# Down pass of three MLP blocks: splits and weight sums all on VectorE, residual rows partly loaded in place, last norm scaled in place

## Chip, core and metric

The kernel runs on one core of one Trainium2 chip. The time is the device time of one execution in microseconds (us). TensorE (PE) does the matmuls into PSUM, VectorE (DVE), ScalarE (ACT) and GpSimd (POOL) do elementwise work, SyncE (SP) issues the DMAs. Each engine works through its own queue in order.

## What is computed

The reference runs three blocks one after the other over an array x of 1024 tokens by 1024 features. Each block is a mixer (attention, recurrence or convolution), an output projection and an MLP with 4096 hidden features; a norm stands behind the last.

```python
# second block; the first has biases b1, b2 and layer norms, the third is built like the second
x = x + mix @ w_out[l]
h = rms_norm_2(x, norm_mlp_g[l])
x = x + jnp.square(jax.nn.relu(h @ w_mlp_up[l])) @ w_mlp_down[l]
...
out = rms_norm_3(h, norm_final_w)      # behind the third block
```

The change touches only the product with w_down (the "down pass") of each of the three MLPs, the step into it, and the final norm.

## The kernel before

`out_mlp` (L1104) is called three times. Every fp32 matrix is kept as a pair, a high part `hi` (a cast by ACT) and a low part `lo = x - hi` (a subtraction), and one product is three matmuls (`mm3`, L219 to L221). Both MLP products are done by a scheme of seven products in place of eight: each operand is a 2 by 2 block matrix, and the seven products take sums of blocks.

The down pass is 28 **stages** j. Stage j belongs to chunk c = j // 7 of the hidden features (four chunks) and to product s = j % 7. A stage has four **tiles** t of 128 tokens, and a tile is 12 matmuls of 128x512 (four k, three matmuls each), so a stage is 48 matmuls. A stage needs:

- its hidden operand `H[j]`, a tile of 1 MB loaded from DRAM two stages ahead by `hload` (L1229) and split in two halves g = 0, 1 by `hsplit` (ACT cast L1234, subtraction L1235). Before, half 0 was subtracted by VectorE and half 1 by GpSimd;
- its weights `W2[j, g]`, split by `wsplit`, which calls `parts` (ACT cast L1100, subtraction on VectorE L1101, written into `wlo`). Products s = 2 to 6 use sums of weight blocks made by `wsums` (L1259 to L1264). The four blocks of a chunk come by `wload` (L1246), 4 MB. `wsums` runs in stages s = 0, 1, 2: eight subtractions of 128x1024 in each chunk. GpSimd did them, apart from the four of the first chunk's s = 0, which VectorE did.

The results lie in PSUM: products s = 0, 2, 4, 6 in the wide tiles `d`, the others in `m` and `s`. `evict(j, t)` adds tile t to X in SBUF (VectorE, L1376); the first one into each place copies with ACT instead (L1379). X has eight rows of 128x1024; a stage adds into rows 0 to 3 or 4 to 7. A matmul of tile t = 2 or 3 in a `d` stage waits for the eviction of tile t - 2 of the same stage. The residual rows `xres` are added in stages s = 3 to 6 of chunks 1 and 2, one row a stage (load L1437, GpSimd add L1438; the first MLP also adds its bias row b2, L1440).

The order of every queue, SyncE's too, is the order in which the code emits the work, forced by `ordered(...)`. Before, `hsplit` and the first `wsplit` of stage j + 1, and all `wsums`, are emitted behind tile 0 of stage j and before that tile's eviction; `wsplit(j + 1, 1)` comes behind tile 1.

The step into the down pass is the 16th round (p = 15) of the up pass, whose last sums (`after(15, 6)`, L1208 to L1213, six instructions on ACT and GpSimd) run during stage 0.

In the last MLP, `done(t, x)` is called behind the evictions of stages 26 and 27, once for each row: square and sum on ACT (L1452, into a scratch tile `st` or `t`), a small step on VectorE (L1453), the power -1/2 on GpSimd (L285), the scaling on VectorE (L1458, written over the scratch tile), and the store to DRAM (L2345). `pipe` runs the square of row t, then the store of row t - 2 and the scaling of row t - 1. There is one `st` and one `t`, used in turn, so the square of row t waits for the store of row t - 2.

Of the kernel before, what the change touches and what calls it, by code (L numbers as in the profile page):

```python
# [102 lines left out]
class K:  # L103
# [1000 lines left out]
    def out_mlp(self, w_out, alpha, norm, w1, b1, w2, b2, done, nxt=None):  # L1104
# [126 lines left out]
        def hsplit(j, g, e):  # L1231
            if j < 28:
                hi, lo = (H[j][:, n, 2 * g : 2 * g + 2] for n in range(2))
                A.copy(hi, f32v(lo))  # L1234
                e.tensor_tensor(lo, f32v(lo), f32v(hi), op=ALU.subtract)  # L1235
# [17 lines left out]
        def wsums(c, s, g):  # L1253

            b11, b12, b21, b22 = w2r[c, g]
            if s == 0:
                t2[g] = (self.st if g else self.t4)().rearrange("p (a b) -> p a b", a=2)
                e = P if c else V
                e.tensor_tensor(b11, b12, b11, op=ALU.subtract)  # L1259
                e.tensor_tensor(t2[g], b22, b11, op=ALU.subtract)  # L1260
            elif s == 1:
                P.tensor_tensor(b12, b22, b12, op=ALU.subtract)
            elif s == 2:
                P.tensor_tensor(b21, b21, t2[g], op=ALU.subtract)  # L1264
# [30 lines left out]
        with self.ordered(("PE", "Activation", "DVE", "Pool", "SP"), False):  # L1295
# [32 lines left out]
            for p in range(1, 16):  # L1328
                for n in range(0 if p > 1 else 2, 7):
# [22 lines left out]
                    else:  # L1352
# [6 lines left out]
                        elif n == 4:  # L1359
                            hsplit(0, 0, V)  # L1360
                            hsplit(0, 1, P)
                            wsplit(0, 0)
                            hload(2)
                        elif n == 5:
                            wsplit(0, 1)
# [6 lines left out]
            def evict(j, t):  # L1372
                q = into[j % 7]
                x = half(q[0], t, q[1])
                if (t, q) in begun:
# [5 lines left out]
            for j in range(28):  # L1381
# [3 lines left out]
                for t in range(4):  # L1385
# [13 lines left out]
                    if t == 0:  # L1399
# [8 lines left out]
                        hsplit(j + 1, 0, V)  # L1408
                        wsplit(j + 1, 0)
                        hsplit(j + 1, 1, P)  # L1410
                        if s < 3:
                            for g in range(2):
                                wsums(c, s, g)
                    if t == 1:
                        wsplit(j + 1, 1)

# [14 lines left out]
                if c in (1, 2) and s >= 3:  # L1431

                    t = 4 * (c - 1) + s - 3
                    if b2 is not None and t == 0:
                        b2t = self.gbtile(b2, self.g3())
                    r = self.slot("qa", [128, 1024], F32)
                    nc.sync.dma_start(out=r, in_=xr[:, t])  # L1437
                    P.tensor_tensor(X[:, t], X[:, t], r, op=ALU.add)  # L1438
                    if b2 is not None:
                        P.tensor_tensor(X[:, t], X[:, t], b2t, op=ALU.add)  # L1440
        self.qp.release()

    def rms_stages(self, t, x, g, end=None):
# [13 lines left out]
        def scale():  # L1457
            nc.vector.scalar_tensor_tensor(out=L["y"], in0=x, scalar=L["rs"], in1=g, op0=ALU.mult, op1=ALU.mult)  # L1458
# [937 lines left out]
```

## Time and profile before

| what | value |
|---|---|
| median of 3 runs | 3884.6 us (3877.1 to 3891.63) |
| the profiled execution's own time | 3888.89 us |
| its span, first to last instruction | 3887.2 us |
| mean granted TensorE clock | 0.952 of full |
| busy share of the span: PE, DVE, POOL, ACT | 91%, 61%, 45%, 39% |
| down passes, stages 0 to 25, three of them | 320.40, 310.70 and 311.09 us |

The three down passes lie at 1185 to 1516, 2350 to 2669 and 3526 to 3870 us of the span. Times below are us from the start of the span. A stage's start is the start of its first matmul in TensorE's timeline. In the rows, `X L1376` is an eviction, `wlo L1101` a weight split, `p L1235` or `q L1235` a split of the hidden operand.

### The profile page before, as it was taken

Reading aid. Unit: us, or ns where it says so; the run is one execution under the profiler, and the core shown is the slowest. Engines: PE = TensorE matmul, PEld = TensorE weight load, DVE = VectorE, ACT = ScalarE, POOL = GpSimd, SP = SyncE. Lnnn points to the kernel's source line nnn. Section 1 sums busy time; section 2 is a strip of 40 time slices with the busy share of each in tenths; the row PEclk is TensorE's granted clock in tenths of the full one; section 3 lists DMA queues with packets and bytes.
Section 4 is the critical chain, followed back from the end, with each engine's and each line's share of the span. In section 5 each row is a group of like instructions: output and inputs, shape, how many; then the busy total and the mean of one; then the engine's idle time right before and its main releaser. Section 6 shows DMA issues by size and latency. Waiting matters only on the chain.

```text
span 3887.2 us, 46771 instructions
## 1 busy us (share of the span) xinstructions
PE 3530.0 (91%) x17908; PEld 2877.7 (74%) x17908; DVE 2376.4 (61%) x3261; ACT 1515.4 (39%) x2485; POOL 1732.0 (45%) x1105
## 2 busy tenths in 40 slices
PE   8898898978999997868989999998999989999997
PEld 7777776766887776667767887776888867887775
DVE  7676534465556777797655556776445345556775
ACT  3333334443444333446733334333422233334332
POOL 2011103255555775577625555673112125555664
PEclk9998898989999998988999999999999999999998
DMA  4221235124456442310124446431111323445442
GB/s 159 63 52 52 61 114 193 60 74 127 150 156 215 154 157 87 78 42 23 38 83 130 150 156 217 168 136 65 48 55 44 104 71 122 150 150 211 152 152 92
DMA packets 335108, 438.51 MB, mean 113 GB/s; under 512 B 44459, under 2 KB 213864, under 8 KB 334244
## 3 DMA queue, kind: packets, MB, share of 16 engines
q1 hardware_dynamic: 331428, 429.23, 33.8%
q10 hardware_dynamic: 3456, 6.29, 0.4%
q8 instruction: 141, 2.31, 0.2%
q14 instruction: 83, 0.68, 0.1%
HBM read 298.62 MB, written 136.84 MB: 112 GB/s over the span
## 4 chain that ended last, share of the span: by engine, by line
PE 62%; DVE 16%; DMA 6%; issue 6%; POOL 5%; ACT 5%; SPq 1%; POOLq 0%; DVEq 0%; ACTq 0%
PE d L219 10%; PE d L221 10%; PE d L220 10%; PE s L219 4%; PE s L220 4%; PE s L221 4%; PE m L219 3%; PE m L220 3%; PE m L221 3%; DVE wlo L1101 3%; DMA L<-Ld 1%; DVE wlo L206 1%; PE s L2187 1%; DVE X L1376 1%; DVE acc L1592 1%
## 5 line engine op out<-in xcount | busy, mean ns | idle before, releaser
L219 PE MATMUL d<-p,whi 128*128 128x512 f32 x960 | 378.1, 394 | 38.9 <-DVE X L1201 27.0
L221 PE MATMUL d<-p,wlo 128*128 128x512 f32 x960 | 370.2, 386 | 4.7 <-DVE wlo L206 4.7
L220 PE MATMUL d<-p,whi 128*128 128x512 f32 x960 | 369.8, 385 | 3.4 <-POOL p L1081 3.4
L219 PE MATMUL d<-whi,p 128*128 128x512 f32 (+1 forms) x864 | 338.7, 392 | 35.4 <-DVE X L1376 25.5
L285 POOL TENSOR_TENSOR col<-col,mhalf 128x1 f32<-128x1 f32 (+2 forms) x132 | 128.8, 977 | 516.1 <-DVE col L1453 221.7
L1183 POOL TENSOR_TENSOR X<-X 128x512 f32<-128x512 f32 x144 | 169.3, 1176 | 400.1 <-ACT X L1182 400.1
L220 PE MATMUL d<-wlo,p 128*128 128x512 f32 (+1 forms) x864 | 327.5, 379 | 9.6 <-DVE wlo L206 8.7
L221 PE MATMUL d<-whi,p 128*128 128x512 f32 (+1 forms) x864 | 326.3, 378 | 2.0 <-DVE p L985 1.3
L219 PEld LDWEIGHTS d<-p,whi 128*128 128x128 f32 x960 | 182.7, 190 | 81.9 <-DVE X L1201 30.9
L219 PEld LDWEIGHTS d<-whi,p 128*128 128x128 f32 x864 | 171.8, 199 | 95.6 <-DVE X L1376 39.4
L1235 POOL TENSOR_TENSOR p<-p 128x1024 fp32r<-128x1024 f32 x54 | 171.0, 3169 | 143.3 <-ACT p L1234 47.8
L1101 DVE TENSOR_TENSOR wlo<-q,whi 128x1024 fp32r<-128x1024 f32 x72 | 214.2, 2975 | 10.2 <-ACT whi L1100 10.2
L1182 ACT ACTIVATE X<-X 128x512 f32<-128x512 f32 x144 | 91.0, 632 | 321.6 <-DVE X L1194 132.8
L221 PEld LDWEIGHTS d<-p,wlo 128*128 128x128 f32 x960 | 182.7, 190 | 43.3 <-DVE wlo L206 5.5
L220 PEld LDWEIGHTS d<-p,whi 128*128 128x128 f32 x960 | 183.0, 191 | 41.2 <-POOL p L1081 4.2
L1101 DVE TENSOR_TENSOR wlo<-raw,whi 128x1024 fp32r<-128x1024 f32 (+1 forms) x90 | 134.3, 1492 | 127.7 <-ACT whi L1100 127.7
L220 PEld LDWEIGHTS d<-wlo,p 128*128 128x128 f32 x864 | 172.3, 199 | 34.6 <-DVE wlo L206 9.4
L221 PEld LDWEIGHTS d<-whi,p 128*128 128x128 f32 x864 | 172.1, 199 | 31.5 <-DVE p L985 2.7
L1100 ACT CAST whi<-q 128x1024 fp32r<-128x1024 f32 x72 | 75.6, 1050 | 298.9 <-PE d L221 163.5
L206 DVE TENSOR_TENSOR wlo<-raw,whi 128x1024 fp32r<-128x1024 f32 (+3 forms) x91 | 121.3, 1337 | 82.1 <-ACT whi L206 81.7
L1376 DVE TENSOR_TENSOR X<-X,d 128x512 f32<-128x512 f32 x156 | 105.1, 680 | 107.7 <-PE d L221 107.7
L220 PE MATMUL m<-wlo,p 128*128 128x512 f32 (+2 forms) x416 | 150.4, 361 | 14.3 <-DVE wlo L1101 14.3
(635 smaller groups left out, 10319.4 us busy)
## 6 DMA issues: line engine op xcount, KB each, us to landing
hd<-X SPq DMA_DIRECT2D x48, 1280.0 KB, 4.8
p<-hd SPq DMA_DIRECT2D x108, 512.0 KB, 4.4
raw<-in_w_in_dram SPq DMA_DIRECT2D x62, 512.0 KB, 4.0
q<-hd SPq DMA_DIRECT2D x60, 512.0 KB, 4.5
hd<-X SPq DMA_DIRECT2D x48, 512.0 KB, 3.5
raw<-in_w_dram SPq DMA_DIRECT2D x32, 512.0 KB, 6.3
xres<-X SPq DMA_DIRECT2D x32, 512.0 KB, 2.6
raw<-in_w_mlp_up_dram SPq DMA_DIRECT2D x32, 512.0 KB, 6.3
```

Of the source, the lines that this page charges most:

```text
L206: self.split = nc.scalar.copy(hi, raw), nc.vector.tensor_tensor(lo, raw, f32v(hi), op=ALU.subtract), ld
L219: mm(out, ah, bh, start=first, stop=False, **kw)
L220: mm(out, ah, bl, start=False, stop=False, **kw)
L221: mm(out, al, bh, start=False, stop=last, **kw)
L285: self.nc.gpsimd.tensor_tensor(out, src, self.mhalf[:, :n], op=ALU.pow)
L1100: nc.scalar.copy(hi, x)
L1101: nc.vector.tensor_tensor(lo, x, f32v(hi), op=ALU.subtract)
L1182: A.activation(h, h, AF.Relu)
L1183: P.tensor_tensor(h, h, h, op=ALU.mult)
L1235: e.tensor_tensor(lo, f32v(lo), f32v(hi), op=ALU.subtract)
L1376: V.tensor_tensor(x, x, out[j, t], op=ALU.add)
L1592: V.scalar_tensor_tensor(out=ac[:, q : q + wd], in0=h[:, q + k : q + k + wd], scalar=cw[:, n, k : k + 1], in1=ac[:, q : q + wd], op0=ALU.m ...
```

## The change

- `hsplit` does all its subtractions on VectorE, and half 1 is emitted behind tile 1 of the stage, not behind tile 0.
- `wsums` runs on VectorE alone, and is emitted behind tiles 2 and 3, so behind the splits of the next stage.
- In the step into the down pass the two first weight splits are emitted one product later (n = 5 and 6, not 4 and 5).
- Residual rows 4 to 7 are loaded by two DMAs of 1 MB straight into X during stage 2, so the first evictions into those rows add (VectorE) and do not copy (ACT). Rows 0 to 3 are still loaded aside and added by a new function `addend`, on VectorE, behind tile 2; the bias row of the first MLP is added on VectorE behind tile 3.
- The last norm scales X in place and stores from X. The scratch tile is then free as soon as its square is done.

```diff
@@ -1228,11 +1228,11 @@
                         c = 4 * (j // 7) + 2 * g
                         nc.sync.dma_start(out=f32v(H[j][:, 1, 2 * g : 2 * g + 2]), in_=hd[j % 7, :, c : c + 2])
 
-        def hsplit(j, g, e):
+        def hsplit(j, g):
             if j < 28:
                 hi, lo = (H[j][:, n, 2 * g : 2 * g + 2] for n in range(2))
                 A.copy(hi, f32v(lo))
-                e.tensor_tensor(lo, f32v(lo), f32v(hi), op=ALU.subtract)
+                V.tensor_tensor(lo, f32v(lo), f32v(hi), op=ALU.subtract)
 
         def wload(c):
             if c < 4:
@@ -1255,13 +1255,27 @@
             b11, b12, b21, b22 = w2r[c, g]
             if s == 0:
                 t2[g] = (self.st if g else self.t4)().rearrange("p (a b) -> p a b", a=2)
-                e = P if c else V
-                e.tensor_tensor(b11, b12, b11, op=ALU.subtract)
-                e.tensor_tensor(t2[g], b22, b11, op=ALU.subtract)
+                V.tensor_tensor(b11, b12, b11, op=ALU.subtract)
+                V.tensor_tensor(t2[g], b22, b11, op=ALU.subtract)
             elif s == 1:
-                P.tensor_tensor(b12, b22, b12, op=ALU.subtract)
+                V.tensor_tensor(b12, b22, b12, op=ALU.subtract)
             elif s == 2:
-                P.tensor_tensor(b21, b21, t2[g], op=ALU.subtract)
+                V.tensor_tensor(b21, b21, t2[g], op=ALU.subtract)
+
+        def addend(c, s, n):
+
+            nonlocal b2t
+            t = 4 * (c - 1) + s - 3
+            if n == 0 and t < 4:
+                r = self.slot("qa", [128, 1024], F32)
+                nc.sync.dma_start(out=r, in_=xr[:, t])
+                V.tensor_tensor(X[:, t], X[:, t], r, op=ALU.add)
+            elif n == 1 and b2 is not None:
+                if t == 0:
+                    b2t = self.gbtile(b2, self.g3())
+                V.tensor_tensor(X[:, t], X[:, t], b2t, op=ALU.add)
+
+        b2t = None
 
 
         first = None
@@ -1357,11 +1371,12 @@
                         elif n == 3:
                             hload(1)
                         elif n == 4:
-                            hsplit(0, 0, V)
-                            hsplit(0, 1, P)
-                            wsplit(0, 0)
+                            hsplit(0, 0)
+                            hsplit(0, 1)
                             hload(2)
                         elif n == 5:
+                            wsplit(0, 0)
+                        elif n == 6:
                             wsplit(0, 1)
 
             half = lambda q, t, c: X[:, 4 * q + t, 512 * c : 512 * c + 512]
@@ -1372,7 +1387,7 @@
             def evict(j, t):
                 q = into[j % 7]
                 x = half(q[0], t, q[1])
-                if (t, q) in begun:
+                if (t, q) in begun or q[0] == 1:
                     V.tensor_tensor(x, x, out[j, t], op=ALU.add)
                 else:
                     begun.add((t, q))
@@ -1405,14 +1420,18 @@
                             wload(1)
                         if s == 0 and c:
                             wload(c + 1)
-                        hsplit(j + 1, 0, V)
+                        hsplit(j + 1, 0)
                         wsplit(j + 1, 0)
-                        hsplit(j + 1, 1, P)
-                        if s < 3:
-                            for g in range(2):
-                                wsums(c, s, g)
-                    if t == 1:
+                    elif t == 1:
+                        hsplit(j + 1, 1)
                         wsplit(j + 1, 1)
+                    elif s < 3:
+                        wsums(c, s, t - 2)
+                    elif c in (1, 2):
+                        addend(c, s, t - 2)
+                    if j == 2 and t in (1, 2):
+                        x = slice(2 * t + 2, 2 * t + 4)
+                        nc.sync.dma_start(out=X[:, x], in_=xr[:, x])
 
                     if j == 1 and t >= 2:
                         evict(0, 2 * t - 4)
@@ -1428,19 +1447,9 @@
                             else:
                                 self.XT[1] = self.xt_meta() if nxt == "meta" else self.xt_half(1)
                         done(t + 4 * (s - 5), X[:, t + 4 * (s - 5)])
-                if c in (1, 2) and s >= 3:
-
-                    t = 4 * (c - 1) + s - 3
-                    if b2 is not None and t == 0:
-                        b2t = self.gbtile(b2, self.g3())
-                    r = self.slot("qa", [128, 1024], F32)
-                    nc.sync.dma_start(out=r, in_=xr[:, t])
-                    P.tensor_tensor(X[:, t], X[:, t], r, op=ALU.add)
-                    if b2 is not None:
-                        P.tensor_tensor(X[:, t], X[:, t], b2t, op=ALU.add)
         self.qp.release()
 
-    def rms_stages(self, t, x, g, end=None):
+    def rms_stages(self, t, x, g, end=None, out=None):
 
         nc = self.nc
         XT = getattr(self, "XT", None)
@@ -1455,7 +1464,7 @@
             self.rpow(L["rs"], ss, 1)
 
         def scale():
-            nc.vector.scalar_tensor_tensor(out=L["y"], in0=x, scalar=L["rs"], in1=g, op0=ALU.mult, op1=ALU.mult)
+            nc.vector.scalar_tensor_tensor(out=L["y"] if out is None else out, in0=x, scalar=L["rs"], in1=g, op0=ALU.mult, op1=ALU.mult)
 
         return [square, scale, lambda: end(L["y"]) if end else self.to_xt(XT, t, L["y"])]
 
@@ -2342,7 +2351,8 @@
         def done(t, x):
             if t == 0:
                 G[1] = self.gbtile(i["norm_final_w_3"], self.g3())
-            self.pipe(*self.rms_stages(t, x, G[1], lambda y: nc.sync.dma_start(out=ov[:, t], in_=y)))
+            q, s, _ = self.rms_stages(t, x, G[1], out=x)
+            self.pipe(q, s, lambda: nc.sync.dma_start(out=ov[:, t], in_=x))
 
         self.out_mlp(i["w_out_3"][0], 1.0, self.rms_feed("norm_mlp_w_3"), i["w_up_3"][0], None, i["w_down_3"][0], None, done)
         self.flush()
```

In each down pass 28 hidden splits and 28 of the 32 weight sums leave GpSimd's queue and stand in VectorE's, with the added rows. The lines of the kernel after shift a little: `wsums` is L1258 to L1263, the eviction L1391, the scaling L1467.

VectorE, third MLP, from the first hidden split for stage 1 on. L1235 is a hidden split, L1101 a weight split, L1259 and L1260 (before) or L1258 and L1259 (after) are weight sums. Before:

```order
L1235 TENSOR_TENSOR p_3784_25725<-p_3784_25725 128x1024
L1101 TENSOR_TENSOR wlo_25811<-q_3782_25687,whi_25810 128x1024
L1259 TENSOR_TENSOR q_3782_25687<-q_3782_25687 128x2x512
L1260 TENSOR_TENSOR t_3794_25816<-q_3782_25687 128x1024
L1259 TENSOR_TENSOR p_3783_25688<-p_3783_25688 128x2x512
L1260 TENSOR_TENSOR st_25819<-p_3783_25688 128x1024
L1101 TENSOR_TENSOR wlo_25835<-p_3783_25688,whi_25834 128x1024
```

And after, the same place:

```order
L1101 TENSOR_TENSOR wlo_25791<-q_3774_25667,whi_25790 128x1024
L1235 TENSOR_TENSOR p_3776_25705<-p_3776_25705 128x1024
L1101 TENSOR_TENSOR wlo_25809<-p_3775_25668,whi_25808 128x1024
L1258 TENSOR_TENSOR q_3774_25667<-q_3774_25667 128x2x512
L1259 TENSOR_TENSOR t_3788_25824<-q_3774_25667 128x1024
L1258 TENSOR_TENSOR p_3775_25668<-p_3775_25668 128x2x512
L1259 TENSOR_TENSOR st_25839<-p_3775_25668 128x1024
```

The four weight sums stood ahead of the second weight split (wlo of the p tile) and now stand behind it; the second hidden split, which was GpSimd's, stands between the two weight splits.

VectorE, third MLP, stages 26 and 27: the end of the kernel's down pass with the first rows of the norm. L1453 and L1462 are the small step, L1458 and L1467 the scaling. Before:

```order
L1235 TENSOR_TENSOR q_3976_27613<-q_3976_27613 128x1024
L1101 TENSOR_TENSOR wlo_27683<-q_3894_26819,whi_27682 128x1024
L1376 TENSOR_TENSOR X_5269<-X_5269,s_27530 128x512
L1453 TENSOR_SCALAR col_27692<-col_27692 128x1
L1101 TENSOR_TENSOR wlo_27710<-p_3895_26820,whi_27709 128x1024
L1376 TENSOR_TENSOR X_5269<-X_5269,m_27555 128x512
L1453 TENSOR_SCALAR col_27715<-col_27715 128x1
L1458 SCALAR_TENSOR_TENSOR st_27691<-X_5269,col_27695,g_3983_27689 128x1024
L1376 TENSOR_TENSOR X_5269<-X_5269,s_27573 128x512
```

And after:

```order
L1101 TENSOR_TENSOR wlo_27653<-q_3886_26801,whi_27652 128x1024
L1391 TENSOR_TENSOR X_5269<-X_5269,s_27500 128x512
L1462 TENSOR_SCALAR col_27660<-col_27660 128x1
L1235 TENSOR_TENSOR q_3964_27583<-q_3964_27583 128x1024
L1101 TENSOR_TENSOR wlo_27680<-p_3887_26802,whi_27679 128x1024
L1391 TENSOR_TENSOR X_5269<-X_5269,m_27523 128x512
L1462 TENSOR_SCALAR col_27685<-col_27685 128x1
L1467 SCALAR_TENSOR_TENSOR X_5269<-X_5269,col_27663,g_3971_27657 128x1024
L1391 TENSOR_TENSOR X_5269<-X_5269,s_27543 128x512
```

The second hidden split now stands between the small step of the first row and the second weight split, and the scaling writes X in place of `st`.

## Rows read from the trace of the kernel before

**Rows 1.** The page: busy time, share of the span and instructions by engine.

```profile
PE 3530.0 (91%) x17908; PEld 2877.7 (74%) x17908; DVE 2376.4 (61%) x3261; ACT 1515.4 (39%) x2485; POOL 1732.0 (45%) x1105
```

**Rows 2.** Windows, stages 0 to 25: us; PE, PEld, DVE, ACT, POOL busy; PEclk; DMA; GB/s.

```profile
1184.86:1505.26 320.40, 297.70 (x1250) 237.98 (x1249) 232.44 (x170) 115.27 (x125) 221.25 (x76) 0.97 0.44 158
2349.57:2660.27 310.70, 293.94 (x1250) 235.59 (x1248) 227.31 (x170) 115.02 (x125) 199.89 (x68) 0.98 0.43 156
3526.38:3837.47 311.09, 294.31 (x1250) 235.86 (x1249) 226.93 (x170) 115.11 (x125) 200.48 (x68) 0.98 0.43 156
```

**Rows 3.** Windows, third pass: stages 1, 2, 3 and 9, same columns.

```profile
3537.57:3558.07 20.50, 13.48 (x49) 10.62 (x48) 17.59 (x8) 7.14 (x10) 14.26 (x5) 0.83 0.89 320
3558.07:3568.96 10.89, 10.89 (x49) 9.01 (x48) 6.02 (x6) 3.61 (x5) 8.20 (x3) 1.00 0.31 98
3568.96:3580.16 11.20, 11.20 (x50) 9.02 (x49) 4.74 (x3) 6.04 (x8) 2.63 (x1) 1.00 0.28 94
...
3635.09:3650.16 15.07, 13.01 (x50) 10.11 (x49) 11.75 (x10) 4.11 (x6) 15.06 (x5) 0.89 0.20 70
```

**Rows 4.** Waits of TensorE, third pass to the end: total, times, longest.

```profile
PE d L219 <- DVE X L1376: 17.4, 16, 7.2
PE s L220 <- DVE wlo L1101: 7.0, 1, 7.0
PE d L219 <- DVE X L1201: 1.3, 1, 1.3
```

**Rows 5.** Timeline of TensorE in stage 1: start, duration, [idle before <- who ended it].

```profile
3546.34 0.79 PE L220 MATMUL s<-wlo,p 128*128 128x512 f32 x1 [7.02 <-DVE wlo L1101]
...
3547.36 0.63 PE L219 MATMUL s<-whi,p 128*128 128x512 f32 x1
```

**Rows 6.** Timeline of VectorE, stages 0 and 1 of the third pass.

```profile
3529.30 1.47 DVE L1235 TENSOR_TENSOR p<-p 128x1024 fp32r<-128x1024 f32 x1 [2.40 <-ACT p L1234]
...
3532.93 2.31 DVE L1259 TENSOR_TENSOR q<-q 128x1024 f32<-128x1024 f32 x1
...
3542.92 3.37 DVE L1101 TENSOR_TENSOR wlo<-p,whi 128x1024 fp32r<-128x1024 f32 x1
```

**Rows 7.** Timeline of GpSimd, same place.

```profile
3528.64 1.04 POOL L1209 TENSOR_TENSOR X<-X 128x512 f32<-128x512 f32 x1
3529.76 2.17 POOL L1210 TENSOR_TENSOR X<-X 128x512 f32<-128x512 f32 x1
...
3538.60 6.61 POOL L1235 TENSOR_TENSOR p<-p 128x1024 fp32r<-128x1024 f32 x2
```

**Rows 8.** Instructions of line 1235: duration in ns, min/median/max, by engine.

```profile
L1235 DVE TENSOR_TENSOR p<-p x54: 1216/1226/3393, 1188.3 to 3826.7; 128x1024 fp32r<-128x1024 f32 x54
L1235 POOL TENSOR_TENSOR p<-p x54: 2393/3326/3405, 1197.3 to 3826.8; 128x1024 fp32r<-128x1024 f32 x54
```

**Rows 9.** Timeline of VectorE: stage 26 and the last eviction.

```profile
3839.41 3.42 DVE L1101 TENSOR_TENSOR wlo<-q,whi 128x1024 fp32r<-128x1024 f32 x1
3842.75 0.67 DVE L1376 TENSOR_TENSOR X<-X,s 128x512 f32<-128x512 f32 x1
...
3846.85 0.68 DVE L1376 TENSOR_TENSOR X<-X,m 128x512 f32<-128x512 f32 x1
...
3876.40 0.68 DVE L1376 TENSOR_TENSOR X<-X,d 128x512 f32<-128x512 f32 x1
```

**Rows 10.** The chain that ended last, one row of the last norm: start, us, what.

```profile
3850.14 2.65 DMA out_dram<-st
...
3852.88 1.16 ACT st L1452 x2
3854.06 0.15 DVE col L1453
3854.21 1.20 DVE t L1458
```

**Rows 11.** Landing of the residual rows' loads (L1437).

```profile
DMA to landing us min/median/max: 5.2/5.3/6.6
```

## The prediction, made before the changed kernel was run

> **What bounds the kernel now.** I read the page first: TensorE is busy for 91% of the span, VectorE 61%, GpSimd 45% [rows 1]. So a gain has to come out of the 9% in which TensorE waits, and the change can reach only the waits in the three down passes, in the step into them and in the last norm. Next I cut each down pass out by windows, from the first matmul of stage 0 to the first of stage 26: 320.40, 310.70 and 311.09 us [rows 2]. Then I cut single stages. An undisturbed stage takes 10.89 us, or 11.20 us where the hidden operand lies in `q`; TensorE is then busy throughout (stages 2 and 3) [rows 3]. Of the 26 stages, 9 are of the `q` kind (every third), so a pass without waits is 17 x 10.89 + 9 x 11.20 = 285.9 us. The three passes stand 34.5, 24.8 and 25.2 us above that, 84.5 us together. This sum is what the change can win in the passes.
>
> Where it lies: stage 1 takes 20.50 us, 9.6 too many [rows 3]. TensorE waits 7.02 us in it for one weight split [rows 5], and afterwards its matmuls take 0.63 us each and the mean granted clock of the stage is 0.83: it works for a while at the lower of its two clocks, 1.2 GHz, and the wait of 7.0 costs 9.6 [rows 3, 5]. The other passes have the like in stage 1, so about 29 of the 84.5 us are these three waits. The rest, some 56 us, is spread over the `d` stages: TensorE waits at `d` tiles for VectorE's evictions [rows 4]; stage 9 with 15.07 us is one of them [rows 3].
>
> Who is late, and why: VectorE does the same subtraction of 128x1024 in 1.22 us at best and in 3.39 at worst, GpSimd in 2.39 to 3.41 [rows 8]. The long ones lie side by side. While GpSimd does sums of 128x512, which take 1.04 by themselves and 2.17 here, VectorE's weight sum takes 2.31, about 1.22 + 1.04; beside GpSimd's splits of the hidden operand (6.61 for two) its weight split takes 3.37 [rows 6, 7]. Each seems to wait for the other's instruction. The page "SBUF — State Buffer" of the Trainium skill (Who interferes with whom) says so: VectorE with two SBUF inputs and GpSimd share a port pair, whoever starts first holds it for its whole instruction, and the other blocks. By that rule work that leaves GpSimd gives VectorE its 1.22 us back at once; the rows agree. In stage 9 GpSimd is busy for 15.06 of the 15.07 us and TensorE for 13.01; in stage 3 GpSimd is busy for 2.63 and nothing waits [rows 3].
>
> **The change part by part.**
>
> *Stage 1.* Before, four weight sums stand ahead of the weight split that TensorE waits for, at 2.3 to 3 us each [rows 6]. After, they stand behind it. I follow the new queue from the hidden split at 3529.30 [rows 6], whose start is set by a load and does not move. Four splits lie there: hidden, weight, hidden, weight. GpSimd's last sums of the up pass stay where they are and last until about 3536 to 3538, so I take 2.31 for each: done by 3538.5. Stage 1 begins at 3537.57 [rows 3] and needs this split half a tile in, about 1.4 us later. Enough, by half a microsecond; with the sums of GpSimd over sooner, by two. I take the whole wait as gone, 9.6 us a pass, 29 in all; if it were late by one full instruction, 3 us a pass would come back with it. The four sums come next, then the splits for stage 2: eight instructions at 1.22 us are 9.8 us, done before stage 2 needs them.
>
> *Step into the pass.* The first weight splits come one product later. Hidden splits no longer go to GpSimd, so the eviction L1201, for which TensorE waits 1.3 us [rows 4], is early. But the second weight split now stands behind ACT's work on the next eviction and comes about as much late for stage 0. I count nothing; the bounds are -1.3 and +1.3 us a pass.
>
> *The other stages.* In stage j VectorE now does four splits for stage j + 1 and four evictions: 4 x 1.22 + 4 x 0.68 = 7.6 us [rows 8, 9]. In s = 1 and s = 2 two weight sums come on top (10.0 us), in s = 0 four (12.5 us), in s = 3 to 6 of chunks 1 and 2 one or two added rows (8.8 to 10.0 us). The rows' durations overlap a little at their ends, so these are upper values. Only s = 0 exceeds the stage's 10.89 us, by 1.6, and the next two stages take it back. TensorE's waits inside a stage need the eviction of tile 0 before tile 2 starts, 5.4 us into the stage: VectorE has the last eviction of the stage before (0.68), two splits (2.44) and this eviction (0.68) to do, 3.8 us. Before, the weight split alone took 3.42 there, beside GpSimd's [rows 9]. The sums come behind tiles 2 and 3, where no matmul of the same stage waits. So these waits go too; I leave 4 us of them for the three passes. No row shows a weight sum on VectorE without GpSimd beside it: the bounds are 1.22 (the split of the same size) [rows 8] and 2.31 [rows 6]. I take 1.22, since the operation, the size and the engine are the same.
>
> *Residual rows.* Twelve loads remain, and now VectorE waits for them in place of GpSimd. A load is issued about 1 us into the stage and lands 5.3 us later [rows 11]; the addition stands behind the eviction of tile 1, which TensorE allows at 5.5. Behind it are the evictions of tiles 2 and 3, for which nobody waits before the next `d` stage. Cost nothing; if the loads came late, 12 times up to 5.3 us, 64 us. The rows 4 to 7 come as 2 MB in stage 2, where DMA is used to 0.31 [rows 3], and are first added in stage 3. The eight evictions a pass that ACT did cost VectorE 8 x 0.68 us in stages 3 and 6; in stage 3 it is busy for 4.74 of 11.20 [rows 3].
>
> *Last norm.* Before, a row goes round in 2.65 (store) + 1.16 (square) + 0.15 + 1.20 (scaling of the row before) and small gaps, 5.27 us, and each square waits for a store [rows 10]. After, it waits for the eviction alone: eviction 0.68, square 1.16, 0.15, scaling 1.20, in all 3.2 us with the gaps. Stage 26 as before: the eviction of tile 0 at 3842.75 [rows 9] comes at 3840.6, since the weight split falls from 3.42 to 1.22; the second hidden split (1.22, and ACT's cast ahead of it, now behind the first square) goes in between; the eviction of tile 1 comes at about 3845.9, where it was at 3846.85 [rows 9]. Six rounds of 3.24 later the last eviction is at 3865.3, where it was at 3876.40 [rows 9]. Behind it all is as before. Gain 11 us. In the first two MLPs the norms behind the pass begin 1 us earlier each for the same reason: 2 us.
>
> *Sum.* 84.5 - 4 + 11 + 2 = 93.5 us. The profiled execution took 3888.89 us, which would become 3795; the median of the runs shown lies 4.3 us below it, so I forecast **3791 us**.
>
> **The rivals.**
>
> *The wait in stage 1 stays.* GpSimd's sums of the up pass are not moved and lie beside exactly these splits. If they stretch the splits past 3539, the wait shrinks but the lower clock comes back with it. Against: half a microsecond or more of room. Without these 29 us the time is 3820.
>
> *Weight sums cost 2.31 on VectorE by themselves.* Then s = 0 comes to 16.8 us and s = 1, 2 to 12.2; the lateness at the `d` stage s = 2 reaches 7.2 us and TensorE waits some 4.7 us there, in twelve chunks 56 us: 3847. For: every row of them is long. Against: each of those rows has GpSimd beside it.
>
> *Residual loads hold VectorE up.* With all of the 64 us above, 3855. Against: 5.3 us [rows 11] fit ahead of the addition.
>
> *VectorE becomes the bound, and the kernel slower.* If the long durations were VectorE's own and not GpSimd's doing, four splits at 3.39 and four evictions would take 16.3 us a stage, 5.4 above TensorE's 10.89; over 78 stages 420 us, about 4300. It decides from a mean of 2.04 us for a split, (10.89 - 2.72) / 4. The page "Perfetto Trace Analysis" (Optimizing Scalar/DVE Operations) gives the rule behind such a fear: where VectorE is saturated, moving work to ScalarE or even GpSimd may help; VectorE is busy for 73% of a pass [rows 2] and this change does the opposite. The same page adds that the shared port may undo it. Against: 1.22 us in the rows whenever GpSimd is idle.
>
> **How the numbers follow.** Forecast 0.74, stage 1 stays 0.11, long weight sums or slow loads 0.09, VectorE the bound 0.03, something else near no change 0.03. Faster by over 0.5% (about 19 us, what a measurement of this kernel can tell from none) holds for all but the last two: 0.94; within 0.5% 0.03; slower 0.03. The range: upwards it takes in the wait of stage 1 (3820) and 2 us of spread between runs, so 3822; downwards the 4 us that I left, 1.3 us a pass in the step, and a run some 7 us below the median, as those shown are: 3775.
>
> **What would show it.** VectorE's L1235, L1101, L1258 to L1263 all near 1.22 us in the passes, but for stage 0; GpSimd idle between the last sum of the up pass and the norm. The stages 0 to 25 at about 287 us a pass; no wait over 1 us at `wlo`. In the end rounds of about 3.2 us and no `out_dram` in the chain but for the last. It would be wrong if the splits stay long without GpSimd beside them, if stage 1 still runs at a granted clock below 1, or if VectorE waits for `qa` or X loads with TensorE waiting behind it.

## The result, and the profile of the changed kernel

| | before | after |
|---|---|---|
| median of the comparison | 3886.59 us (4 runs, 3877.1 to 3891.63) | 3769.85 us (4 runs, 3766.07 to 3780.07) |
| profiled execution | 3888.89 us, span 3887.2 | 3767.91 us, span 3766.2 |
| stages 0 to 25, three passes | 320.40, 310.70, 311.09 us [rows 2] | 287.20, 287.11, 287.12 us |
| start of stage 26 to the end of the span | 49.7 us | 36.2 us |

The ratio is 0.9707, 95% interval 0.9679 to 0.9734: faster, by more than forecast. 3769.85 lies 21 us below the 3791 of the prediction and 5 below its range.

The page's first line, then windows over stages 0 to 25 of the three passes and over single stages of the third (0, 1, 9), answer to [rows 1, 2, 3]:

```profile
PE 3483.8 (93%) x17908; PEld 2855.3 (76%) x17908; DVE 2364.7 (63%) x3473; ACT 1504.9 (40%) x2461; POOL 1121.7 (30%) x905
...
1167.86:1455.06 287.20, 286.36 (x1250) 234.22 (x1249) 233.85 (x244) 112.72 (x118) 9.59 (x6) 1.00 0.50 178
2294.05:2581.16 287.11, 286.35 (x1249) 234.21 (x1248) 224.22 (x236) 112.45 (x117) 9.69 (x6) 1.00 0.47 171
3442.91:3730.03 287.12, 286.36 (x1250) 234.23 (x1249) 225.54 (x236) 112.42 (x117) 10.58 (x6) 1.00 0.48 172
...
3442.91:3455.39 12.48, 11.71 (x50) 8.94 (x48) 9.44 (x5) 6.95 (x8) 10.58 (x6) 1.00 0.91 338
3455.39:3466.29 10.90, 10.90 (x49) 9.01 (x48) 10.83 (x11) 7.00 (x9) 0.00 (x0) 1.00 1.00 354
...
3544.00:3555.19 11.19, 11.19 (x49) 9.02 (x48) 9.38 (x12) 4.04 (x6) 0.00 (x0) 1.00 0.27 94
```

VectorE does 236 to 244 instructions in a pass where it did 170, and is busy for no longer: 224 to 234 us against 227 to 232 [rows 2]. GpSimd's 200 to 221 us are 10. TensorE waits 0.8 us a pass, all in stage 0; the granted clock is 1.00 throughout.

The waits of TensorE in the third pass, and the instructions of L1235 (ns, min/median/max), answer to [rows 4, 8]:

```profile
PE d L220 <- DVE wlo L1101: 0.8, 1, 0.8
...
L1235 DVE TENSOR_TENSOR p<-p x108: 1216/1219/2317, 1173.2 to 3722.8; 128x1024 fp32r<-128x1024 f32 x108
L1235 DVE TENSOR_TENSOR q<-q x60: 1218/1218/1227, 1161.4 to 3735.9; 128x1024 fp32r<-128x1024 f32 x60
```

VectorE across stages 0 and 1 (timeline: start, duration), to be held against [rows 6]:

```profile
3451.20 2.32 DVE L1235 TENSOR_TENSOR p<-p 128x1024 fp32r<-128x1024 f32 x1
3453.44 2.31 DVE L1101 TENSOR_TENSOR wlo<-p,whi 128x1024 fp32r<-128x1024 f32 x1
3455.68 1.21 DVE L1258 TENSOR_TENSOR q<-q 128x1024 f32<-128x1024 f32 x1
3456.92 1.23 DVE L1259 TENSOR_TENSOR t<-q 128x1024 f32<-128x1024 f32 x1
```

The weight split for which TensorE waited 7 us is done 0.4 us into stage 1, still at 2.31 beside GpSimd's last sums. The weight sums behind it take 1.21 to 1.23.

### The profile page after: what moved, and what is told of

It reads as the page before. It is cut to its first block, busy times and chain, and to the rows that moved or that the text cites. A ratio compares the mean times of both kernels' runs of the same rounds, so it can differ in the third digit from the quotient of the medians.

```text
span 3766.2 us, 46503 instructions
## 1 busy us (share of the span) xinstructions
PE 3483.8 (93%) x17908; PEld 2855.3 (76%) x17908; DVE 2364.7 (63%) x3473; ACT 1504.9 (40%) x2461; POOL 1121.7 (30%) x905
## 3 DMA queue, kind: packets, MB, share of 16 engines
q8 instruction: 141, 2.31, 0.3%
## 4 chain that ended last, share of the span: by engine, by line
PE 73%; DVE 11%; ACT 4%; DMA 4%; issue 4%; POOL 3%; SPq 0%; POOLq 0%; DVEq 0%; ACTq 0%
PE d L219 13%; PE d L221 13%; PE d L220 13%; PE s L219 5%; PE s L221 5%; PE s L220 5%; PE m L219 4%; PE m L220 4%; PE m L221 4%; DMA L<-Ld 1%; PE s L2196 1%; DVE wlo L206 1%; DVE acc L1601 1%; POOL st L1595 1%; DVE t L1601 1%
## 5 line engine op out<-in xcount | busy, mean ns | idle before, releaser
L219 PE MATMUL d<-whi,p 128*128 128x512 f32 (+1 forms) x864 | 332.5, 385 | 8.4 <-DVE X L1727 3.6
L221 PE MATMUL d<-whi,p 128*128 128x512 f32 (+1 forms) x864 | 324.1, 375 | 2.3 <-DVE p L985 1.3
L1101 DVE TENSOR_TENSOR wlo<-raw,whi 128x1024 fp32r<-128x1024 f32 (+1 forms) x90 | 135.8, 1508 | 128.7 <-ACT whi L1100 128.7
L206 DVE TENSOR_TENSOR wlo<-raw,whi 128x1024 fp32r<-128x1024 f32 (+3 forms) x91 | 120.1, 1324 | 81.0 <-ACT whi L206 80.5
L1391 DVE TENSOR_TENSOR X<-X,d 128x512 f32<-128x512 f32 x168 | 114.8, 684 | 83.2 <-PE d L221 83.1
L1234 ACT CAST p<-p 128x1024 fp32r<-128x1024 f32 x108 | 113.4, 1050 | 118.1 <-DMA p<-hd 118.1
L206 ACT CAST whi<-raw 128x1024 fp32r<-128x1024 f32 (+3 forms) x91 | 94.1, 1040 | 155.8 <-PE d L220 46.2
L219 PE MATMUL m<-whi,p 128*128 128x512 f32 (+2 forms) x416 | 150.9, 363 | 1.5 <-DVE q L1066 1.0
```

What stands on the lines that cost most here:

```text
L206: self.split = nc.scalar.copy(hi, raw), nc.vector.tensor_tensor(lo, raw, f32v(hi), op=ALU.subtract), ld
L219: mm(out, ah, bh, start=first, stop=False, **kw)
L221: mm(out, al, bh, start=False, stop=last, **kw)
L1101: nc.vector.tensor_tensor(lo, x, f32v(hi), op=ALU.subtract)
L1391: V.tensor_tensor(x, x, out[j, t], op=ALU.add)
```

## The experiments

All times stand beside the kernel before on the same chip. Line numbers shift by a few lines from kernel to kernel (the eviction is L1376, L1390 to L1396). The passes column is the sum of stages 0 to 25 over the three passes; "tail" runs from the start of stage 26 to the end of the span.

| kernel | median us | ratio to before (95%) | passes us | tail us |
|---|---|---|---|---|
| before, again | 3875.48 | 0.9999 (0.9986 to 1.0012) | 941.9 | 49.7 |
| engine alone | 3904.36 | 1.0071 (1.0047 to 1.0094) | 986.2 | 48.5 |
| order, residual rows, norm; GpSimd still at work | 3843.23 | 0.9911 (0.9889 to 0.9933) | 931.0 | 37.4 |
| norm alone | 3863.95 | 0.9961 (0.9949 to 0.9973) | 942.0 | 37.4 |
| engine, sums behind | 3815.39 | 0.9816 (0.9792 to 0.9839) | 882.2 | 48.5 |
| after, again | 3769.63 | 0.9707 (0.9688 to 0.9727) | 861.4 | 36.2 |
| after + idle work on GpSimd | 3815.38 | 0.9826 (0.9804 to 0.9849) | 901.2 | 36.2 |
| after, one split back | 3770.75 | 0.9716 (0.9690 to 0.9743) | 861.5 | 36.2 |
| after, all rows loaded apart | 3770.88 | 0.9715 (0.9692 to 0.9737) | 861.4 | 36.2 |
| after + earlier splits, deeper norm | 3763.14 | 0.9691 (0.9671 to 0.9711) | 857.4 | 30.9 |
| the same, again | 3764.28 | 0.9694 (0.9674 to 0.9715) | 857.4 | 30.9 |

### The kernel before, again: where the base went wrong

No edit.

> The kernel before, unchanged, profiled once more. It asks whether the stretch of low clock in front of the passes (granted clock 0.50 from 410 to 430 us, TensorE busy throughout, 11 to 15 us lost) belongs to this kernel or to one execution. Theory A, chance: this execution shows 1.00 there, or shows the drop elsewhere, and its span lies 10 to 15 us off that of the first profile. Theory B, tied to the kernel: 0.50 again in the same place, pass 1 entered at 1185 us as before (1167.86 in the changed kernel). Passes either way 320, 311 and 311 us.

Windows of the first profile of before, then of this one, at 362 to 364, 364 to 366 and 410 to 420 us:

```profile
362.00:364.00 2.00, 2.00 (x10) 0.50 0.04 8
364.00:366.00 2.00, 2.00 (x8) 0.50 0.00 0
410.00:420.00 10.00, 10.00 (x96) 0.50 0.35 101
...
362.00:364.00 2.00, 2.00 (x15) 1.00 0.00 0
364.00:366.00 2.00, 2.00 (x15) 1.00 0.00 0
410.00:420.00 10.00, 9.62 (x83) 1.00 0.30 105
```

The columns are length, PE busy (count), granted clock, DMA share, GB/s. Theory A holds: the same program, span 3871.7 in place of 3887.2, and 14.4 of the 15.5 us lie in front of pass 1 (stage 0 at 1170.43, not 1184.86). Of 13 profiled executions four show the stretch at 0.50 near 405 to 432 us: two of kernels with the old passes, one with the sums behind, one of the fastest kernel. Of 44 runs of before, 29 took 3871 to 3880 us and 15 took 3884 to 3892, with none between. That the upper group is the stretch is likely but seen in two profiled runs only: 3888.89 us with it, 3873.47 without.

### The changed kernel, again

> The changed kernel once more, beside the kernel before on the same chip. The first comparison set a profile of before with 27 us at a granted clock of 0.50 in front of the passes against one of after without. Theory: that stretch comes and goes from one execution to the next whatever the kernel; then the median of before is near 3876 and that of after near 3766 to 3768 again, ratio 0.971 to 0.973, and passes of 287.1 to 287.2 us each. Rival: the change itself removes the stretch; then no execution of it ends 10 us or more above its fastest.

3769.63 us and passes of 287.1 to 287.2. The rival falls: one run of the first comparison ended 14 us above the fastest (3780.07 against 3766.07), and the stretch occurs in a profile of the fastest kernel, which holds the whole change.

### The engine alone

```diff
-                e = P if c else V
+                e = V
...
-                P.tensor_tensor(b12, b22, b12, op=ALU.subtract)      # the like for b21 and the added rows
+                V.tensor_tensor(b12, b22, b12, op=ALU.subtract)
...
-                        hsplit(j + 1, 1, P)
+                        hsplit(j + 1, 1, V)
```

> Of the change only the engine: all splits, weight sums and added rows go to VectorE, in the order of the kernel before; residual loads and the last norm as before. Theory A (the long VectorE instructions are two engines waiting for each other's): outside stage 0 the splits L1235 and L1101 and the weight sums take 1.22 us; the evictions of most stages are early, but the sums now stand in the queue ahead of the second weight split and the next evictions: four sums in s = 0 are 4.9 us, so stage 1 and the stages s = 1 and 2 keep a wait of some 2 to 4 us. About a third to two thirds of the 81 us of the passes: 3830 to 3860. Theory B (the durations are VectorE's own): splits stay near 2 to 3.4 us, VectorE becomes the bound, above 4000.

3904 us, 28 slower than before: outside both theories. The durations are as A says. Stage 7 of the third pass: VectorE's timeline, TensorE's matmul behind its wait, the stage's window, and last the same stage of the kernel before, from its second profile:

```profile
3618.18 1.22 DVE L1235 TENSOR_TENSOR p<-p 128x1024 fp32r<-128x1024 f32 x1
3619.32 1.22 DVE L1259 TENSOR_TENSOR q<-q 128x1024 f32<-128x1024 f32 x1
...
3622.96 1.22 DVE L1260 TENSOR_TENSOR st<-p 128x1024 f32<-128x1024 f32 x1
3624.11 0.68 DVE L1376 TENSOR_TENSOR X<-X,d 128x512 f32<-128x512 f32 x1
...
3624.84 0.80 PE L219 MATMUL d<-whi,p 128*128 128x512 f32 x1 [5.10 <-DVE X L1376]
...
3614.14:3633.09 18.95, 13.85 (x50) 10.86 (x48) 11.23 (x11) 6.45 (x8) 0.00 (x0) 0.82 0.76 277
...
3597.82:3608.81 10.99, 10.99 (x49) 8.93 (x48) 7.00 (x6) 5.33 (x6) 7.15 (x3) 1.00 0.91 333
```

Every split and every sum takes 1.22 us, GpSimd does nothing, and the stage is 8 us longer than before. Three splits and four sums stand ahead of the eviction of tile 0, which comes 10 us into the stage, while TensorE needs it at 5.4; TensorE waits 5.1 us, and the stage's mean granted clock falls to 0.82. I had counted on waits of 2 to 4 us in stage 1 and in the stages s = 1 and 2, not on one in s = 0 itself, and left out what the clock adds. Stages 7, 14 and 21 do this in each pass.

### The order alone

The code of after, but with GpSimd for `hsplit(j, 1)`, the sums (chunk 0, s = 0 apart) and the added rows:

```diff
-                V.tensor_tensor(lo, f32v(lo), f32v(hi), op=ALU.subtract)
+                (P if g else V).tensor_tensor(lo, f32v(lo), f32v(hi), op=ALU.subtract)
```

> Of the change only the order, the residual rows in place and the last norm in place; GpSimd does half of the hidden splits, the weight sums (but those of chunk 0, s = 0) and the added rows, as before. Theory A: the wait for the weight split in stage 1 goes (10.9 us for the stage), 29 us for three passes, and the end gains its 13; beside GpSimd the splits stay long (up to 3.4 us) and the d stages keep most of their 52 us of waits: about 3840 to 3850. Rival: the order alone does it, and passes come to 287 us with GpSimd still at work: near the changed kernel's 3770.

3843.23 us, as theory A has it. Of the 33 us 12 are the norm. Stage 1 is down from 20 to 11 or 12 us, but stage 2 rises by 3 to 6 and stage 0 by 1, and the others keep their waits. Stage 9 of the third pass, VectorE and the window:

```profile
3604.38 2.90 DVE L1235 TENSOR_TENSOR p<-p 128x1024 fp32r<-128x1024 f32 x1
3607.20 3.42 DVE L1101 TENSOR_TENSOR wlo<-q,whi 128x1024 fp32r<-128x1024 f32 x1
3610.55 0.68 DVE L1392 TENSOR_TENSOR X<-X,d 128x512 f32<-128x512 f32 x1
...
3603.57:3618.53 14.96, 13.01 (x49) 10.07 (x48) 11.47 (x7) 3.98 (x5) 12.62 (x5) 0.89 0.20 70
```

### The weight sums behind the splits

The engine-alone kernel with one move:

```diff
-                        if s < 3:
-                            for g in range(2):
-                                wsums(c, s, g)
                     if t == 1:
                         wsplit(j + 1, 1)
+                    if t > 1 and s < 3:
+                        wsums(c, s, t - 2)
```

> The kernel before with all of this work on VectorE, and, unlike the first such kernel (3904 us), the weight sums queued behind tiles 2 and 3 in place of ahead of the second weight split; first splits, residual loads and the last norm as before. If the place of the sums is what spoilt the engine's gain, stages 7, 14 and 21 come from 18.7 to 20.5 us back to about 11, stage 1 from 18 to 11, and 9, 16 and 23 to 11.2 or less: passes of 288 to 295 us, in all 3785 to 3805. Rival: the rest of the old order (hidden split of the second half ahead of the eviction, residual rows) keeps waits of a like size: above 3830.

Passes of 299.16, 291.49 and 291.51 us, the first above the 288 to 295 expected: 104 us of passes gained by this one move. Stage 7, 18.95 us in the engine-alone kernel, takes 11.51 (first line below). The time is 10 us above the expected; its profile has the stretch at 0.50, and one of its four runs took 3802. What is left over shows two lesser places. In stages 4 and 7 the first split starts late because ScalarE copies an eviction before its cast, and TensorE waits 0.31 us in stage 4. In stage 11 a residual row stands in front of the splits, and TensorE waits 0.48 (1.74 in pass 1, where a bias row stands there as well):

```profile
3552.46:3563.97 11.51, 11.20 (x49) 8.93 (x48) 9.71 (x10) 6.45 (x8) 0.00 (x0) 1.00 0.92 335
...
3597.74 1.22 DVE L1437 TENSOR_TENSOR X<-X,qa 128x1024 f32<-128x1024 f32 x1
3598.88 1.22 DVE L1235 TENSOR_TENSOR q<-q 128x1024 fp32r<-128x1024 f32 x1
```

### Work on GpSimd that nobody needs

After, with a subtraction of 128x1024 on GpSimd that changes no result (one a stage in pass 2, two in pass 3):

```diff
+        def junk(j, g):
+            y = self.g3().rearrange("p (a b) -> p a b", a=2)
+            hi = f32v(H[j][:, 0, 2 * g : 2 * g + 2])
+            P.tensor_tensor(y, hi, hi, op=ALU.subtract)
```

> The changed kernel with useless subtractions of 128x1024 on GpSimd, whose result nobody reads and whose buffer no other work waits for in that time: none in pass 1, one a stage in pass 2, two a stage in pass 3 (stages 1 to 23). Theory A (VectorE and GpSimd block each other's instructions): VectorE's splits beside them take up to 3.4 us in place of 1.22, and TensorE's waits come back though all of the change's order stands: pass 1 at 287.2, pass 2 about 292 to 305, pass 3 295 to 325 us. Theory B (the order of the queues alone was the cause): 287 us in all three.

Windows of the three passes, then VectorE and GpSimd around the start of stage 9 of the third:

```profile
1167.17:1454.37 287.20, 286.35 (x1249) 234.25 (x1248) 233.19 (x244) 112.71 (x118) 9.60 (x6) 1.00 0.49 177
2293.74:2586.68 292.94, 289.97 (x1249) 232.34 (x1248) 257.34 (x236) 112.43 (x117) 71.05 (x29) 1.00 0.46 168
3449.81:3770.89 321.08, 299.72 (x1249) 238.62 (x1248) 286.18 (x236) 112.46 (x117) 135.53 (x52) 0.97 0.42 153
...
3558.54 5.39 POOL L1283 TENSOR_TENSOR g<-p 128x1024 f32<-128x1024 f32 x2 [4.88 <-ACT p L1234]
...
3559.27 0.67 DVE L1396 TENSOR_TENSOR X<-X,s 128x512 f32<-128x512 f32 x1
3559.86 2.31 DVE L1261 TENSOR_TENSOR p<-p 128x1024 f32<-128x1024 f32 x1
3562.10 0.68 DVE L1396 TENSOR_TENSOR X<-X,m 128x512 f32<-128x512 f32 x1
3562.70 2.31 DVE L1235 TENSOR_TENSOR p<-p 128x1024 fp32r<-128x1024 f32 x1
```

Theory A. Pass 1 is a control in the same execution. VectorE does the same 236 instructions in passes 2 and 3 and is busy 33 and 61 us longer than in after; TensorE pays 5.8 and 34.0 us. The second piece of work a stage costs nearly five times the first; most of the first seems to fall into VectorE's free time, since 33 us more of VectorE's work cost TensorE 5.8. Two kinds of VectorE instructions stand beside the same GpSimd work here: those that read two operands from SBUF take 2.31 in the lines shown and 2.92 at most in passes 2 and 3, not the 3.4 expected; the evictions, which read one from PSUM, keep 0.67 to 0.69 throughout. The page "SBUF — State Buffer" of the Trainium skill (Who interferes with whom) draws the line just there, at two SBUF inputs; the trace agrees.

### Two parts of the order taken back

```diff
                         wsplit(j + 1, 0)
+                        hsplit(j + 1, 1)
                     elif t == 1:
-                        hsplit(j + 1, 1)
                         wsplit(j + 1, 1)
```

> The changed kernel with one instruction put back in its old place: the split of the hidden operand's second half stands before the eviction of tile 0 again, still on VectorE. VectorE then has the last eviction of the stage before, three splits and this eviction ahead of TensorE's tile 2, 0.68 + 3 x 1.22 + 0.68 = 5.0 us of the 5.4. Theory: too tight with the gaps: TensorE waits 0.3 to 0.5 us in most d stages, as in the kernel with the sums behind (0.31 in stages 4 and 7), each wait costs 0.6 to 0.8 us with the clock after it, and the passes take 290 to 292 us. Rival: 5.0 is less than 5.4 and nothing waits: 287.1.

The rival: 287.21, 287.11 and 287.13 us. 5.0 us fit into 5.4.

```diff
-            if n == 0 and t < 4:
+            if n == 0:
...
-                if (t, q) in begun or q[0] == 1:
+                if (t, q) in begun:
...
-                        nc.sync.dma_start(out=X[:, x], in_=xr[:, x])
```

> The changed kernel with all eight residual rows a pass loaded into a buffer and added, none in place; so 24 additions on VectorE in place of 12, and ScalarE makes the first copy of four half rows again. Theory: the rows stand behind tiles 2 and 3, where VectorE has room in each of those stages; nobody waits: passes of 287.1 to 287.3 us, time as the changed kernel's 3768. Rival: the loads in place are what frees the d stages of chunk 2 (11, 13 and 18 to 21 waited 0.3 to 1.7 us with VectorE doing the rows at the stage's end): 289 to 295 us a pass.

The theory: 287.19, 287.12 and 287.10 us. Either part can be taken back at no cost. Where the same split place and the same copies by ScalarE come together, in stages 4 and 7 of the kernel with the sums behind, they cost 0.6 us a stage (0.31 us of waiting in stage 4).

### The last norm alone

```diff
...
-            self.pipe(*self.rms_stages(t, x, G[1], lambda y: nc.sync.dma_start(out=ov[:, t], in_=y)))
+            q, s, _ = self.rms_stages(t, x, G[1], out=x)
+            self.pipe(q, s, lambda: nc.sync.dma_start(out=ov[:, t], in_=x))
```

> The kernel before with the last norm written in place, nothing else. From the start of stage 26 to the end the changed kernel gained 13.6 us. If the buffer of the store alone is the cause of that, this kernel shows about 11 to 14 us of it: rounds of 3.2 us in place of 5.27 and no wait for a store but the last: 3873 to 3876. If the first eviction's weight split (3.4 us beside GpSimd) holds the tail as well, 2 us less. Passes as before, 320, 311 and 311 us.

The tail is 37.4 us, 12.3 less than in before, with the long first weight split still there; after has 36.2. The other 1.2 us come with the engine: the order with GpSimd at work keeps 37.4, the engine alone takes 1.2 off before's tail. By medians the norm gains 12.8 us; 3863.95 is below the expected 3873 to 3876, which had been reckoned from the higher base of the first comparison.

### A version that is faster than both

```diff
                             hload(1)
+                            hsplit(0, 0)
                         elif n == 4:
-                            hsplit(0, 0)
                             hsplit(0, 1)
+                            wsplit(0, 0)
                             hload(2)
                         elif n == 5:
-                            wsplit(0, 0)
-                        elif n == 6:
                             wsplit(0, 1)
...
+            nc.scalar.activation(y, x, AF.Square, accum_out=ss)
+            if t:
+                root(t - 1)
+            if t > 1:
+                scale(t - 2)
+            if t == 7:
+                root(7)
+                scale(6)
+                scale(7)
```

`root` is the sum's scaling and power, `scale` the scaling in place and the store.

> The changed kernel with two edits. (1) The splits for stage 0 one product earlier, so that neither L1201 nor the weight split of stage 0 is late: 1.3 us in each of three passes, stage 0 at 11.2 us in place of 12.5. (2) The last norm one step deeper: VectorE no longer waits 1.22 to 1.28 us a row for the square that was just issued, but prepares the row before and scales the one before that, 2.1 us of work a row; TensorE's 2.8 us a tile would then set the rounds (3.22 before), stage 27 would come from 15.06 to about 11.2 to 12 us, and the last eviction 5 us earlier. Together about 9 us: 3757 to 3760. Rival for (2): the chain square, root, scale of one row sets the rounds anyway, and nothing is won there: 3763.

> The changed kernel with earlier first splits and the deeper last norm once more, for a narrower time: passes of 285.8 us, 31.0 us from the start of stage 26 to the end, 36.2 in the changed kernel, together 9 us less than that; the median 3758 to 3763, as the stretches of low clock in front of the passes fall.

A round of the last norm in after, from eviction to eviction, then one in this kernel, and this kernel's stage 27; last, from stage 26 of pass 1 to stage 0 of pass 2, the window of after and that of this kernel:

```profile
3751.06 0.68 DVE L1391 TENSOR_TENSOR X<-X,d 128x512 f32<-128x512 f32 x1
3753.02 0.15 DVE L1462 TENSOR_SCALAR col<-col 128x1 f32<-128x1 f32 x1 [1.28 <-ACT t L1461]
3753.09 1.28 DVE L1467 SCALAR_TENSOR_TENSOR X<-X,col,g 128x1024 f32<-128x1024 f32 x1
3754.28 0.68 DVE L1391 TENSOR_TENSOR X<-X,d 128x512 f32<-128x512 f32 x1
...
3749.73 0.69 DVE L1390 TENSOR_TENSOR X<-X,d 128x512 f32<-128x512 f32 x1 [0.86 <-PE d L221]
3750.33 0.15 DVE L2370 TENSOR_SCALAR col<-col 128x1 f32<-128x1 f32 x1
3750.40 1.27 DVE L2375 SCALAR_TENSOR_TENSOR X<-X,col,g 128x1024 f32<-128x1024 f32 x1
3752.53 0.69 DVE L1390 TENSOR_TENSOR X<-X,d 128x512 f32<-128x512 f32 x1 [0.86 <-PE d L221]
...
3743.93:3755.29 11.36, 11.36 (x49) 8.83 (x47) 8.26 (x13) 4.83 (x10) 7.06 (x5) 1.00 0.46 185
...
1455.06:2294.05 838.99, 729.18 (x3545) 594.65 (x3543) 551.54 (x762) 390.12 (x710) 464.86 (x356) 0.93 0.30 91
1456.50:2297.64 841.14, 731.95 (x3545) 597.40 (x3544) 553.26 (x763) 391.11 (x711) 465.58 (x356) 0.92 0.29 91
```

VectorE waits for TensorE now, not for ScalarE's square; rounds of 3.22 us are 2.80, the tail is 30.9 us and the passes are at their floor, 285.8. By windows that is 9.2 us, as expected. But the medians, 3763.1 and 3764.3, lie above the 3757 to 3760 and 3758 to 3763 expected, and the medians of 8 runs each differ by 5.4 only (3769.6, 3764.3). Some 2 us of this recur: from stage 26 of pass 1 to stage 0 of pass 2 both profiles of this kernel take 841.1 us, and the five of after and of the kernels made from it above (idle work, one split back, rows apart) 839.0 to 839.5, although the round in front of the pass takes 19.37 us in all of them. Why is open, and so is what the clock in front of the passes adds.

## Why the prediction was right in its parts and too high in its time

The mechanism held; sizes failed. The base stood 6.5 us too high. The sum was 7.5 us too small in its own terms: 3.9 in the 4 us of waits left for the `d` stages, 2.5 in the last norm, 0.8 in the step, the rest in the other norms. A further 4.5 us lie in code on which it put no term. Together that is 18.5 of the 21 us; the other 3 lie between the profiles and the medians of the runs.

**Stage 1: right, cause and size.** 10.9 us in each pass. The split was done 0.4 us into the stage, where 1.4 was allowed. The rival fell. The order alone removes the wait and hands it on to stage 2; engine and sums behind remove it altogether, without the later first splits. Two readings were a little off: the four sums ahead of the split took 2.20 to 3.24 us, not 2.3 to 3, and GpSimd's last sum ended at 3538.6, not by 3538. Neither changes the term.

**The other stages: mis-sized by 3.9.** I left 4 us of waits in the `d` stages. They have none: stages 1 to 25 of the three passes are 84.4 us shorter, forecast 80.5. That the passes still stand 3.7 us above three times 285.9 is 1.3 a pass in stage 0, where TensorE waits 0.8 us for the second weight split. I had named that lateness and set it off against the eviction L1201.

**Step into the pass: counted 0, measured 0.8.** The wait for L1201 did go, 1.3 to 1.4 us in front of each pass. With it gone, the round in front of the pass (84 matmuls), which took 20.9 to 21.0 us, takes 19.37, a gain of 1.6 a pass; stage 0 gives 1.3 of it back.

**Weight sums and residual loads: right.** 1.21 to 1.23 us without GpSimd; both rivals fell. That VectorE gets its 1.22 us back at once is right for the durations. But it is worth nothing without the sums' new place, on which the prediction put no price outside stage 1: the engine alone is 28 us slower than before. The rival on the slower side asked for VectorE's mean to exceed the stage; in fact it is enough that seven instructions at 1.22 us stand ahead of one eviction.

**Last norm: short by 2.5.** The tail is 13.5 us shorter, forecast 11. Rounds are 3.22 us, forecast 3.24, and the last eviction comes 11.4 us earlier in the tail, forecast 11.1. "Behind it all is as before" failed. In before the last square waited for a store as well, 2.1 us:

```profile
3879.20 1.06 ACT L1452 ACTIVATE t<-X 128x1024 f32<-128x1024 f32 x1 [4.12 <-DMA out_dram<-t]
```

In after, all that follows the last eviction takes 8.7 us in place of 10.8. The norms behind the other two passes gained 1.0 and 1.2 in stage 26, forecast 1 each.

**The base: wrong.** The sum of 93.5 us was subtracted from a profiled execution with 27 us at half clock in front of the passes, and 4.3 less was called the median of before. The runs were too few to show two groups; the median of 44 is 3878.1. From there 93.5 gives 3784.6 and the range would begin near 3769, barely below the measured 3769.6. (The range's own terms, 4, 3.9 and 7 us, give a lower end of 3776, not 3775.) Two profiles without the stretch, 3871.7 and 3766.2, differ by 105.5 us: 80.5 in the passes, 13.5 in the tail, 4.8 in the steps, 2.2 in the two norms. The other 4.5 lie in code that is the same in both. About half of them recur. From stage 26 of pass 1 to stage 0 of pass 2 three profiles with the old passes take 844.1 to 844.3 us, those five 839.0 to 839.5; step and norm explain 2.6 of these 5. The window in the second profile of before, to be held against that of after above:

```profile
1490.39:2334.52 844.13, 731.26 (x3544) 596.58 (x3543) 555.29 (x761) 391.09 (x710) 470.69 (x358) 0.93 0.29 91
```

Why the part that recurs goes with the change stays open. In front of pass 1 profiles of kernels that share after's code there differ by 3.6 us among themselves, so what lies there can't be put down to the change.

The first pair of profiles differs by 121.0 us, of which 14.7 lie in front of 890 us. A reader of that pair alone would have credited them to the change.

## What to carry to other kernels

Moving work off an engine that blocks another, and the place of that work in the new queue, are one edit: in the passes the engine alone costs 44 us here, the order alone gives 11, both together 80. Count what stands ahead of the instruction that the bound engine needs, not how busy the queue's engine is. Before forecasting a few per cent, look in the profile for stretches of low clock that no wait explains, and ask of each whether the next execution will have it.

## What the runs showed of the hardware

- TensorE's granted clock fell from 1.00 to 0.50 (2.4 to 1.2 GHz) near 405 us in four of 13 executions and stayed there for some 27 us, with TensorE busy 97 to 100% of 370 to 404 us and 98 to 100% of 404 to 432; ahead of the fall it had waited 0.6 us, as it did without a fall. In these four the clock had also come back later after the 9 us wait at 351 us: it was still 0.50 from 364 to 366 us, where the nine others show 0.95 to 1.00. What ties the two together was not tried.
- A VectorE subtraction of 128x1024 with two operands in SBUF took 1.22 us alone, 2.31 to 2.92 beside the idle work on GpSimd, and up to 3.43 in the order alone, where GpSimd did half of the hidden splits and most weight sums; an eviction that reads PSUM took 0.67 to 0.69 in all three cases.
- A wait of 5.1 us cost a stage 8 us, since TensorE went on at a granted clock that averaged 0.82 over that stage; one of 0.31 us cost 0.6, at a granted clock of 1.00.
